# Spreading one row of the first chunk unevenly over the DMA engines, and loading the bias on 16 partitions

## The chip, the cores and the metric

The kernel runs on one core of a Trainium2 chip. The metric is the device time of one execution in microseconds, the median of several runs. A profile is one separate execution, recorded by the hardware; its span runs from the first to the last instruction and is somewhat shorter than the run's time.

## What is computed

A relative position bias is added to attention logits, and a softmax is taken over each row. Everything is float32; there are 2 x 8 matrices of 2112 x 2112.

```python
B, H, S = (2, 8, 2112)
max_rel = 16
rel = pos[:, None] - pos[None, :]
rel_clipped = np.clip(rel, -max_rel, max_rel) + max_rel
bias = rel_bias[:, rel_clipped].copy()          # rel_bias: 8 heads x 33 values
logits = logits + bias[None, :, :, :]
logits = logits - logits.max(axis=-1, keepdims=True)
exp = np.exp(logits)
return (exp / exp.sum(axis=-1, keepdims=True)).astype(np.float32)
```

The bias depends only on the head and on how far a column lies from the row: one of 33 values within 16 columns of the diagonal, and the first or the last of the 33 beyond.

## The kernel before

**Tiling.** All 33792 rows are split over 128 partitions, 264 consecutive rows to each. Eight partitions make one matrix (one batch and head), so partition p belongs to head (p/8) mod 8. A chunk is six rows of every partition (`R = 6`): 128 pieces of 50688 bytes, 6.49 MB. There are 44 chunks and four buffers `X[0]` to `X[3]`, used in turn. A chunk is loaded into a buffer, worked on in place, and stored from it.

**The work of a chunk.** DVE adds the bias and takes the row's maximum in one instruction per row (`add`, L166). ACT takes the exponential with that maximum and sums the row (`exps`, L175). DVE takes the reciprocals of three sums and scales three rows (`scale`, L183 and L187). The bias comes from `F`, a strip of 2135 columns, which DVE copies out of a wider table `M` in PSUM once per four chunks (`strip`, L160); every row reads it at another offset.

**The queues.** SP issues all loads and stores of chunks (`load` L78, `store` L82), in one order written out by hand: first the loads of chunks 0 to 3, then in a loop the store of chunk n+1, a wait until the store of chunk n has landed, and the load of chunk n+4 into the buffer that has become free. The last chunk is stored in two halves. Each transfer raises a semaphore by 16 when all of its parts have landed; `take` waits for a count and subtracts it. A transfer is cut up among 16 DMA engines, which work through their parts in order.

**The start.** The first chunk is not loaded by one transfer but by six, one for each row, over all 128 partitions (L88); the first five raise `pre`, the sixth `ld[0]`. The 8 x 33 bias values are loaded by ACT's queue into the beginning of `F`, the same 264 values on every partition (L97). POOL makes partition and head numbers (L101, L102), DVE makes masks from them (L118 to L128), then waits for the bias (L129), keeps the own head's 33 values with a mask (L131) and adds over the heads (L135), so that `rbS` holds the 33 values of the partition's head; from them it builds the table `M` (L139 to L155). All of these raise one semaphore, `dve`, and `settle` waits until all issued so far are done. Before its loop DVE waits for the five rows (`take(v, pre, ...)`, L190), copies the first strip (L160), waits for the sixth row (L163) and begins to add.

Of the kernel before, what the change touches and what calls it, by code (L numbers as in the profile page):

```python
# [15 lines left out]
def kernel(  # L16
# [6 lines left out]
    nc = tc.nc  # L23
    P = 128
    B, H, S, S2 = logits.shape
    assert S == S2
    MR = 16
    W = 2 * MR + 1
    ROWS = B * H * S // P
    PB = S // ROWS  # L30
    assert ROWS * P == B * H * S and PB * ROWS == S and PB == H == 8
    R = 6
    NBUF = 4
# [4 lines left out]
    MW = S + ROWS - 1  # L38
    FW = S + STEP - 1
    BIG = 3.0e38  # L40

    io = ctx.enter_context(tc.tile_pool(name="io", bufs=1))
    X = [io.tile([P, R * S], FP32, tag=f"X{b}", name=f"X{b}") for b in range(NBUF)]
    F = io.tile([P, FW], FP32, tag="F", name="F")
    rbS = io.tile([P, W], FP32, tag="rbS", name="rbS")
# [3 lines left out]
    ip = io.tile([P, 3, PB], I32, tag="ip", name="ip")  # L49
# [3 lines left out]
    def view(t, offset, dims):  # L53

        return bass.AP(tensor=t.tensor, offset=t.offset + offset, ap=[[list(t.ap[0])[0], P]] + dims)

    def rows(t, j, n):

        return bass.AP(tensor=t.tensor, offset=t.offset + j * S, ap=[[ROWS * S, P], [1, n * S]])

    with tc.tile_critical(no_gpsimd_drain=True):
        ld = [nc.alloc_semaphore(f"ld{b}") for b in range(NBUF)]
# [3 lines left out]
        scaled = nc.alloc_semaphore("scaled")  # L66
        inv = nc.alloc_semaphore("inv")
        rb = nc.alloc_semaphore("rb")
        pre = nc.alloc_semaphore("pre")
        idx = nc.alloc_semaphore("idx")  # L70
        dve = nc.alloc_semaphore("dve")

        def take(eng, sem, n):
            eng.wait_ge(sem, n).then_inc(sem, -n)  # L74


        def load(j, b):
            nc.sync.dma_start(out=X[b][:, :], in_=rows(logits, j, R)).then_inc(ld[b], 16)  # L78
# [5 lines left out]
            ).then_inc(st[b], 16)  # L84


        for r in range(R):
            nc.sync.dma_start(  # L88
                out=X[0][:, r * S : (r + 1) * S], in_=rows(logits, r, 1)
            ).then_inc(ld[0] if r == R - 1 else pre, 16)  # L90
        for n in range(1, NBUF):
            load(n * R, n)

        rbB = view(F, 0, [[1, H * W]])
        nc.scalar.dma_start(  # L97
            out=rbB,
            in_=bass.AP(tensor=rel_bias.tensor, offset=rel_bias.offset, ap=[[0, P], [1, H * W]]),
        ).then_inc(rb, 16)  # L100
        nc.gpsimd.iota(ip[:, 0], pattern=[[0, PB]], base=0, channel_multiplier=1).then_inc(idx, 1)  # L101
        nc.gpsimd.iota(ip[:, 2], pattern=[[1, PB]], base=0, channel_multiplier=0).then_inc(idx, 1)  # L102

        v = nc.vector
        done = [0]

        def then(ins):
            done[0] += 1
            ins.then_inc(dve, 1)

        def settle():
            v.wait_ge(dve, done[0])

        SC = H * W
        mask = [F[:, SC + i * PB : SC + (i + 1) * PB] for i in range(9)]
        dp, dh, eq, hm, gt, le, lt, ra, rz = mask
        v.wait_ge(idx, 2)
        then(v.tensor_scalar(out=ip[:, 1], in0=ip[:, 0], scalar1=3, scalar2=7,  # L118
                             op0=ALU.logical_shift_right, op1=ALU.bitwise_and))
# [7 lines left out]
        for m, op in ((eq, ALU.is_equal), (gt, ALU.is_gt), (le, ALU.is_le), (lt, ALU.is_lt)):  # L127
# [4 lines left out]
            out=view(F, 0, [[W, H], [1, W]]), in0=view(F, 0, [[W, H], [1, W]]),  # L132
            in1=view(F, SC + 3 * PB, [[1, H], [0, W]]), op=ALU.mult))
        settle()
        then(v.tensor_reduce(out=rbS[:, :], in_=view(F, 0, [[1, W], [W, H]]),  # L135
                             axis=mybir.AxisListType.X, op=ALU.add))
        settle()
        low, high = rbS[:, W - 1 : W], rbS[:, 0:1]
        then(v.tensor_scalar(out=ra, in0=gt, scalar1=low, scalar2=None, op0=ALU.mult))  # L139
        then(v.tensor_scalar(out=rz, in0=gt, scalar1=low, scalar2=None, op0=ALU.mult))  # L140
        then(v.tensor_tensor(  # L141
            out=view(F, 0, [[W, PB], [1, W]]), in0=view(F, SC + 2 * PB, [[1, PB], [0, W]]),
            in1=view(rbS, W - 1, [[0, PB], [-1, W]]), op=ALU.mult))
# [6 lines left out]
            out=view(M, U, [[ROWS, PB], [1, W]]), in0=view(F, 0, [[W, PB], [1, W]]),  # L150
            in1=view(F, SC + 8 * PB, [[1, PB], [0, W]]), op=ALU.add))
        then(v.tensor_copy(out=view(M, U + W, [[ROWS, PB], [1, ROWS - W]]),  # L152
                           in_=view(F, SC + 7 * PB, [[1, PB], [0, ROWS - W]])))
        then(v.tensor_copy(out=M[:, 0:U], in_=low.to_broadcast([P, U])))  # L154
# [7 lines left out]
        def add(b):  # L162
            take(v, ld[b], 16)  # L163
            for r in range(b * R, (b + 1) * R):
                x = X[b][:, (r - b * R) * S : (r - b * R + 1) * S]
                v.tensor_tensor_reduce(  # L166
                    out=x, in0=x, in1=F[:, STEP - 1 - r : STEP - 1 - r + S], scale=-1.0, scalar=BIG,
                    op0=ALU.add, op1=ALU.min, accum_out=nmax[:, r : r + 1],
# [18 lines left out]
                    v.tensor_scalar_mul(out=x, in0=x, scalar1=rec[:, r : r + 1]).then_inc(scaled, 1)  # L187

        v.sem_inc(dve, -done[0])
        take(v, pre, 16 * (R - 1))  # L190
        with nc.Fori(0, ROWS - STEP + 1, STEP, engines=[ENG.DVE]) as j:  # L191
            strip(j)
            take(v, dve, 1)
# [51 lines left out]
```

## Time and profile before

| | us |
|---|---|
| Median of 3 runs (1331.09 to 1331.68) | 1331.55 |
| Span of the profiled execution | 1327.7 |
| DVE busy | 976.6 |
| ACT busy | 575.2 |

The profiled execution's own time is not listed beside its span; the runs' median lies 3.85 us above the span. The span is read together with how busy the 16 DMA engines are: the profile gives their mean share and the bytes moved in any window. A packet is what one engine moves in one piece (here one partition's part of a transfer) and is counted in the window in which it starts. In windows of 2 us and less, a long packet at a border shifts the share noticeably. "SPq" and "ACTq" are the instruction queues of SP and ACT, from which transfers are issued.

### The profile page before, as it was taken

The page shows a single profiled execution, that of the slowest core. Times are in us where ns is not written, and L with a number is a line of the kernel's source. Part 1 is how long each engine was busy: PE and PEld are TensorE (multiplying, and loading weights), DVE is VectorE, ACT ScalarE, POOL GpSimd, SP SyncE. Part 2 cuts the span into 40 slices and gives each one's busy share as a digit, 9 for nine tenths or more (in the row PEclk, how much of TensorE's full clock was granted, in tenths as well). Part 3 has the DMA queues.
Part 4 walks back from the last instruction along what each step waited for, and adds up shares of the span by engine and source line. Part 5 has one row for each costly group of instructions (what it writes and reads, how often), then busy time and mean ns, then how long its engine had stood idle before and what let it go on. Part 6 is the DMA issues. An engine that isn't in the chain of part 4 may idle for free. (4 is left out here: it accounts for less than half of the span.)

```text
span 1327.7 us, 2454 instructions
## 1 busy us (share of the span) xinstructions
DVE 976.6 (74%) x911; ACT 575.2 (43%) x539; POOL 0.4 (0%) x6
## 2 busy tenths in 40 slices
DVE  6999667777777776687778777677877776687772
ACT  2564333444444343345444333444444343335440
POOL 0000000000000000000000000000000000000000
DMA  9999999999999999999999999999999999999998
GB/s 392 431 428 437 435 420 437 435 434 425 435 437 434 428 435 434 435 429 429 438 438 432 426 438 437 437 425 437 437 437 425 435 440 437 428 432 438 437 426 359
DMA packets 13683, 571.11 MB, mean 430 GB/s; under 512 B 1521, under 2 KB 1649, under 8 KB 1649
## 3 DMA queue, kind: packets, MB, share of 16 engines
q1 hardware_dynamic: 13536, 570.96, 99.6%
q10 hardware_dynamic: 144, 0.14, 0.1%
q14 instruction: 3, 0.02, 0.0%
HBM read 285.61 MB, written 285.47 MB: 430 GB/s over the span
## 5 line engine op out<-in xcount | busy, mean ns | idle before, releaser
L166 DVE CUSTOM_DVE_ANT_0 X<-X,F 128x2112 f32<-128x2112 f32 x264 | 605.2, 2354 | 301.3 <-DVEq L74 301.3
L175 ACT ACTIVATE X<-X,nmax 128x2112 f32<-128x2112 f32 x264 | 541.7, 2052 | 539.3 <-ACTq L74 517.6
L187 DVE TENSOR_SCALAR X<-X,rec 128x2112 f32<-128x2112 f32 x264 | 332.4, 1315 | 13.2
L175 ACT ACT_TABLE_LOAD x11 | 14.1, 1283 | 183.3 <-ACTq L74 183.3
L175 ACT ACTIVATION_READ_ACCUMULATOR X<-X,nmax 128x1 f32 x264 | 49.2, 186 | 0.0
L160 DVE COPY F<-M 128x2135 f32 x11 | 26.1, 2374 | 6.3 <-DVEq L74 6.3
L166 DVE DVE_READ_ACCUMULATOR2_ANT nmax<- 128x1 f32 x264 | 21.7, 82 | 0.0
L183 DVE RECIPROCAL rec<-tot 128x3 f32<-128x3 f32 x88 | 14.9, 170 | 0.0
L131 DVE TENSOR_TENSOR F<-F 128x264 f32<-128x264 f32 x1 | 0.4, 434 | 4.7 <-DMA F<-in_rel_bias_dram 4.7
L152 DVE COPY M<-F 128x1848 f32<-128x1848 f32 x1 | 2.1, 2077 | 0.0
L118 DVE TENSOR_SCALAR ip<-ip 128x8 int32<-128x8 int32 x1 | 0.2, 173 | 1.3 <-POOL ip L102 1.3
L135 DVE TENSOR_REDUCE rbS<-F 128x33 f32<-128x264 f32 x1 | 0.6, 610 | 0.0
L149 DVE TENSOR_TENSOR M<-F 128x264 f32<-128x264 f32 x1 | 0.4, 441 | 0.0
L141 DVE TENSOR_TENSOR F<-F,rbS 128x264 f32<-128x264 f32 x1 | 0.4, 425 | 0.0
L128 DVE TENSOR_SCALAR F<-F 128x8 f32<-128x8 f32 x4 | 0.4, 166 | 0.0
L154 DVE COPY M<-rbS 128x247 f32<-128x247 f32 x1 | 0.4, 408 | 0.0
L139 DVE TENSOR_SCALAR F<-F,rbS 128x8 f32<-128x8 f32 x1 | 0.2, 231 | 0.0
L145 DVE SCALAR_TENSOR_TENSOR F<-F,rbS 128x8 f32<-128x8 f32 x1 | 0.2, 225 | 0.0
L140 DVE TENSOR_SCALAR F<-F,rbS 128x8 f32<-128x8 f32 x1 | 0.2, 222 | 0.0
L146 DVE SCALAR_TENSOR_TENSOR F<-F,rbS 128x8 f32<-128x8 f32 x1 | 0.2, 219 | 0.0
L124 DVE TENSOR_TENSOR F<-ip 128x8 f32<-128x8 int32 x1 | 0.2, 167 | 0.0
L121 DVE TENSOR_TENSOR F<-ip 128x8 f32<-128x8 int32 x1 | 0.2, 166 | 0.0
(9 smaller groups left out, 1.2 us busy)
## 6 DMA issues: line engine op xcount, KB each, us to landing
X<-in_logits_dram SPq DMA_DIRECT2D x43, 6336.0 KB, 44.6
out_dram<-X SPq DMA_DIRECT2D x43, 6336.0 KB, 52.6
X<-in_logits_dram SPq DMA_DIRECT2D x6, 1056.0 KB, 12.1
out_dram<-X SPq DMA_DIRECT2D x2, 3168.0 KB, 21.1
F<-in_rel_bias_dram ACTq DMA_DIRECT2D x1, 132.0 KB, 6.2
```

The lines of the kernel that those rows point to most:

```text
L128: then(v.tensor_scalar(out=m, in0=dp, scalar1=0.0, scalar2=None, op0=op))
L131: then(v.tensor_tensor(out=view(F, 0, [[W, H], [1, W]]), in0=view(F, 0, [[W, H], [1, W]]), in1=view(F, SC + 3 * PB, [[1, H], [0, W]]), op= ...
L135: then(v.tensor_reduce(out=rbS[:, :], in_=view(F, 0, [[1, W], [W, H]]), axis=mybir.AxisListType.X, op=ALU.add))
L141: then(v.tensor_tensor(out=view(F, 0, [[W, PB], [1, W]]), in0=view(F, SC + 2 * PB, [[1, PB], [0, W]]), in1=view(rbS, W - 1, [[0, PB], [-1, ...
L149: then(v.tensor_tensor(out=view(M, U, [[ROWS, PB], [1, W]]), in0=view(F, 0, [[W, PB], [1, W]]), in1=view(F, SC + 8 * PB, [[1, PB], [0, W]] ...
L152: then(v.tensor_copy(out=view(M, U + W, [[ROWS, PB], [1, ROWS - W]]), in_=view(F, SC + 7 * PB, [[1, PB], [0, ROWS - W]])))
L154: then(v.tensor_copy(out=M[:, 0:U], in_=low.to_broadcast([P, U])))
L160: v.tensor_copy(out=F[:, :], in_=M[:, bass.ds(ROWS - STEP - j, FW)]).then_inc(dve, 1)
L166: v.tensor_tensor_reduce(out=x, in0=x, in1=F[:, STEP - 1 - r : STEP - 1 - r + S], scale=-1.0, scalar=BIG, op0=ALU.add, op1=ALU.min, accum_ ...
L175: nc.scalar.activation(out=x, in_=x, func=EXP, scale=-1.0, bias=nmax[:, r : r + 1], accum_out=tot[:, r : r + 1],).then_inc(expd, 1)
L183: v.reciprocal(out=rec[:, r0 : r0 + HALF], in_=tot[:, r0 : r0 + HALF]).then_inc(inv, 1)
L187: v.tensor_scalar_mul(out=x, in0=x, scalar1=rec[:, r : r + 1]).then_inc(scaled, 1)
```

## The change

The bias is loaded on 16 partitions, one in eight, in place of 128. For that, DVE first clears the 264 columns of `F` on all partitions, and ACT waits for it before it issues the load. The mask and the sum over the heads work as before, and give zeros on partitions without data. Two 32 x 32 block transposes with a copy between them then spread the 33 values of each of the 16 partitions over its group of eight.

The first five rows of the first chunk are one transfer (42240 bytes for each partition), raising `pre`. The sixth row goes in 16 transfers over neighbouring partitions, of 15, 14, and so on down to 8, again 8, and down to 1 partitions. The first eight of them raise `pre`, the next seven `fan`, and the last `ld[0]`. DVE waits for the first two semaphores before its loop, for the last where it waited before. The loads of chunks 1 to 3 follow behind these on SP.

```diff
+    FAN = [15, 14, 13, 12, 11, 10, 9, 8, 8, 7, 6, 5, 4, 3, 2, 1]
...
-        for r in range(R):
-            nc.sync.dma_start(
-                out=X[0][:, r * S : (r + 1) * S], in_=rows(logits, r, 1)
-            ).then_inc(ld[0] if r == R - 1 else pre, 16)
-        for n in range(1, NBUF):
-            load(n * R, n)
-        rbB = view(F, 0, [[1, H * W]])
-        nc.scalar.dma_start(
-            out=rbB,
-            in_=bass.AP(tensor=rel_bias.tensor, offset=rel_bias.offset, ap=[[0, P], [1, H * W]]),
-        ).then_inc(rb, 16)
...
+        then(v.memset(F[:, 0 : H * W], 0.0))
+
+        nc.scalar.wait_ge(dve, 1)
+        nc.scalar.dma_start(
+            out=bass.AP(tensor=F.tensor, offset=F.offset, ap=[[PB * list(F.ap[0])[0], P // PB], [1, H * W]]),
+            in_=bass.AP(
+                tensor=rel_bias.tensor, offset=rel_bias.offset, ap=[[0, P // PB], [1, H * W]]
+            ),
+        ).then_inc(rb, 16)
+        nc.sync.dma_start(
+            out=X[0][:, 0 : (R - 1) * S], in_=rows(logits, 0, R - 1)
+        ).then_inc(pre, 16)
+        p = 0
+        for i, k in enumerate(FAN):
+            nc.sync.dma_start(
+                out=X[0][p : p + k, (R - 1) * S : R * S],
+                in_=bass.AP(
+                    tensor=logits.tensor, offset=logits.offset + (p * ROWS + R - 1) * S,
+                    ap=[[ROWS * S, k], [1, S]],
+                ),
+            ).then_inc(ld[0] if i == len(FAN) - 1 else pre if i < len(FAN) // 2 else fan, 16)
+            p += k
+        for n in range(1, NBUF):
+            load(n * R, n)
...
+        Q = 32
+        RB, RT, RC, RW = [SC + 9 * PB + 2 * Q * i for i in range(4)]
+        then(v.memset(F[:, RB : RB + 2 * Q], 0.0))
...
-        then(v.tensor_reduce(out=rbS[:, :], in_=view(F, 0, [[1, W], [W, H]]),
+        then(v.tensor_reduce(out=F[:, RB : RB + W], in_=view(F, 0, [[1, W], [W, H]]),
                              axis=mybir.AxisListType.X, op=ALU.add))
+        settle()
+        then(v.transpose(out=F[:, RT : RT + 2 * Q], in_=F[:, RB : RB + 2 * Q]))
+        settle()
+        then(v.tensor_copy(out=view(F, RC, [[Q, 2], [PB, Q // PB], [1, PB]]),
+                           in_=view(F, RT, [[Q, 2], [PB, Q // PB], [0, PB]])))
+        settle()
+        then(v.transpose(out=F[:, RW : RW + 2 * Q], in_=F[:, RC : RC + 2 * Q]))
+        settle()
+        then(v.tensor_copy(out=rbS[:, :], in_=F[:, RW : RW + W]))
...
-        take(v, pre, 16 * (R - 1))
+        take(v, pre, 16 * (1 + len(FAN) // 2))
+        take(v, fan, 16 * (len(FAN) - len(FAN) // 2 - 1))
```

More of the change, by code (lines that the diff above doesn't have):

```diff
@@ L40 @@
     BIG = 3.0e38
+    FAN = [15, 14, 13, 12, 11, 10, 9, 8, 8, 7, 6, 5, 4, 3, 2, 1]
+    assert sum(FAN) == P
     io = ctx.enter_context(tc.tile_pool(name="io", bufs=1))
@@ L68 @@
         rb = nc.alloc_semaphore("rb")
-        pre = nc.alloc_semaphore("pre")
         idx = nc.alloc_semaphore("idx")
         dve = nc.alloc_semaphore("dve")
+        pre = nc.alloc_semaphore("pre")
+        fan = nc.alloc_semaphore("fan")
         def take(eng, sem, n):
@@ L84, in store @@
             ).then_inc(st[b], 16)
-        for r in range(R):
-            nc.sync.dma_start(
-                out=X[0][:, r * S : (r + 1) * S], in_=rows(logits, r, 1)
-            ).then_inc(ld[0] if r == R - 1 else pre, 16)
-        for n in range(1, NBUF):
-            load(n * R, n)
-        rbB = view(F, 0, [[1, H * W]])
-        nc.scalar.dma_start(
-            out=rbB,
-            in_=bass.AP(tensor=rel_bias.tensor, offset=rel_bias.offset, ap=[[0, P], [1, H * W]]),
-        ).then_inc(rb, 16)
-        nc.gpsimd.iota(ip[:, 0], pattern=[[0, PB]], base=0, channel_multiplier=1).then_inc(idx, 1)
-        nc.gpsimd.iota(ip[:, 2], pattern=[[1, PB]], base=0, channel_multiplier=0).then_inc(idx, 1)
         v = nc.vector
@@ L112, in settle @@
             v.wait_ge(dve, done[0])
+        then(v.memset(F[:, 0 : H * W], 0.0))
[21 more added lines that the diff above has]
+            load(n * R, n)
+        nc.gpsimd.iota(ip[:, 0], pattern=[[0, PB]], base=0, channel_multiplier=1).then_inc(idx, 1)
+        nc.gpsimd.iota(ip[:, 2], pattern=[[1, PB]], base=0, channel_multiplier=0).then_inc(idx, 1)
         SC = H * W
```

## The prediction, made before the change was run

> **What bounds the kernel now.** I read the page's queue table first, then the waits, then windows of the span, then the start and the end instruction by instruction.
>
> ```profile
> span 1327.7 us, 2454 instructions
> DVE 976.6 (74%) x911; ACT 575.2 (43%) x539; POOL 0.4 (0%) x6
> q1 hardware_dynamic: 13536, 570.96, 99.6%
> q10 hardware_dynamic: 144, 0.14, 0.1%
> ...
> 60.00:1300.00 1240.00, 926.29 (x853) 548.67 (x514) 0.00 (x0) 1.00 1.00 433
> ```
>
> The last row is a window: length, busy time of DVE, ACT and POOL, clock, DMA share, GB/s. SP's queue (q1) keeps the 16 DMA engines busy 99.6% of the span, and from 60 to 1300 us their share is 1.00 at 433 GB/s, which is 27.06 GB/s for one engine. So one row of one partition (8448 bytes) costs an engine 0.312 us, and eight of them, an engine's part of one row of a chunk, 2.50 us. DVE and ACT are never the bound; what they do matters only where it leaves the queue empty. The time is therefore the time of the DMA engine that ends last: start, its bytes, and what it loses on the way. The tail shows how unequal they are:
>
> ```profile
> 1300.00:1320.60 20.60, 3.60 (x3) 0.00 (x0) 0.00 (x0) 1.00 1.00 431
> 1320.60:1321.50 0.90, 0.00 (x0) 0.00 (x0) 0.00 (x0) 1.00 0.40 169
> 1321.50:1324.00 2.50, 0.00 (x0) 0.00 (x0) 0.00 (x0) 1.00 0.45 193
> 1324.00:1325.40 1.40, 0.00 (x0) 0.00 (x0) 0.00 (x0) 1.00 0.21 91
> 1325.40:1326.30 0.90, 0.00 (x0) 0.00 (x0) 0.00 (x0) 1.00 0.00 0
> ```
>
> At 1320.6 us the share falls from 1.00 to 0.40 to 0.45: nine engines have taken their last packet, seven go on, and the last packet is taken before 1325.4. Packets count where they start; those of the last stores (3168 KB over 128 partitions, a row further down) last 25344/27060 = 0.94 us, so the last engine ends near 1326.3, some 5.4 us behind the first. An average engine is 0.40 x 0.9 + 0.45 x 2.5 + 0.21 x 1.4 = 1.8 us behind the first. No view says which of the 16 lag, or when they fell behind. The other loss is at the start:
>
> ```profile
> 0.92 0.41 ACTq L97 DMA_DIRECT2D F<-in_rel_bias_dram  x1
> 0.97 3.34 SPq L88 DMA_DIRECT2D X<-in_logits_dram  x6
> 4.36 1.74 SPq L78 DMA_DIRECT2D X<-in_logits_dram  x3
> ...
> 2.27:4.00 1.73, 0.19 (x3) 0.00 (x0) 0.00 (x0) 1.00 0.99 189
> 4.00:6.00 2.00, 0.00 (x0) 0.00 (x0) 0.00 (x0) 1.00 0.87 280
> 6.00:8.00 2.00, 0.81 (x2) 0.00 (x0) 0.00 (x0) 1.00 0.96 396
> 7.00:19.00 12.00, 5.45 (x12) 0.00 (x0) 0.00 (x0) 1.00 1.01 428
> ```
>
> Against 433 GB/s the first three windows lose 1.73 x (1 - 189/433) + 2 x (1 - 280/433) + 2 x (1 - 396/433) = 0.97 + 0.71 + 0.17 = 1.85 us of every engine. That is when the bias's 128 small packets (q10) run between those of the first row.
>
> **The bias load: 16 packets for 128.** Its 0.14 MB cost 0.14/433 = 0.3 us of all engines; seven eighths go, 0.28 us. If the small packets also caused the 1.85 us beside them, 2.1 us go; if that is only cold starting, none of it. I take 1.2, midway, and keep 0.3 and 2.1. One transfer in place of five saves five rows x 2.50 x (433/428 - 1) = 0.15 us; sixteen transfers end in more semaphore packets and give that back. Sum at the start: -1.2 us for every engine.
>
> **The bias on DVE: nothing.** ACT's issue now waits for a memset of 264 columns. No row shows a memset on DVE; between 0.17 us (8 columns) and 2.08 us (1848) I take the copy of 247 columns, 0.41. A second memset of 64, two transposes of 64 and two copies come on, between 0.17 and 0.43 us each by the narrow rows and L131, so some 1.5 us in all (1.2 to 2.6).
>
> ```profile
> 7.16 0.43 DVE L131 TENSOR_TENSOR F<-F 128x264 f32<-128x264 f32 x1 [4.69 <-DMA F<-in_rel_bias_dram]
> ...
> 9.75 2.08 DVE L152 COPY M<-F 128x1848 f32<-128x1848 f32 x1
> 11.74 0.41 DVE L154 COPY M<-rbS 128x247 f32<-128x247 f32 x1
> 12.06 0.17 DVE L155 COPY M<-rbS 128x16 f32<-128x16 f32 x1
> 18.48 2.38 DVE L160 COPY F<-M 128x2135 f32 x1 [6.26 <-DVEq L74]
> ```
>
> A bias packet may also stand behind two of the first transfer's packets (42240 bytes, 1.56 us each), 3 us more. What hides it all is the 6.26 us that DVE waits before L160 for the first five rows. Those, and the sixth with them now, come no sooner than 15 us, and the setup ends near 12.2 + 0.5 + 1.5, 17 at worst. With the cover gone it costs DVE alone, which has 26% to spare.
>
> **SP's issues: nothing.** Six take 3.34 us, 0.56 each. The loads of chunks 1 to 3 (L78) are moved behind 17 issues: 0.97 + 17 x 0.56 = 10.5 us in place of 4.36. The engines have the five rows until about 2.3 + 12.5 = 14.8 us. An issue would have to cost 0.8 us before an engine ran dry, and those that would run dry first are the ones given fewest packets.
>
> **The sixth row: the term that decides.** Engine 0 is to take 16 packets in place of 8, engine 15 none. At its own pace engine 0 gains 8 x 0.312 = 2.5 us of work, engine 15 loses as much, and the others lie between. That holds if 27.06 GB/s belongs to the engine. Before, every transfer goes over all 128 partitions, so the trace cannot tell the pace of an engine from the pace of the part of SBUF that it writes: 128/16 is eight partitions to a part. If the pace is the part's, fifteen neighbouring partitions written by fifteen engines crowd into few parts, each with one engine's pace to share. How many of a block lie in one part: at least 1, at most 8. I take 4. A packet then costs up to 4 x 0.312 = 1.25 us. Engine 4 is in the twelve transfers of five partitions and more; crowded throughout they cost it 15.0 us, never crowded 3.7. Stepping through all engines' packets in order, with equal shares in a part and the next load's packets taking shares too, I get 12.7 us for engine 4, the worst, against 2.5 before: **+10.2 us**. The same steps give +6.2 with two to a part and +14.9 with eight, and these are my ends. Engine 15 comes out at 0: it runs ahead into chunk 1 and loses that lead to engines which write into its part. [...]
>
> [...]
>
> **What is late next.** The first strip waits for the sixth row now, behind it all of DVE's first chunk, then ACT, then SP's store: at about 14.8 + 12.7 = 27.5 us in place of 18.48, 9 us later.
>
> ```profile
> 43.07 22.23 SPq L82 DMA_DIRECT2D out_dram<-X  x2
> 81.12 0.36 SPq L78 DMA_DIRECT2D X<-in_logits_dram  x1
> ...
> X<-in_logits_dram SPq DMA_DIRECT2D x43, 6336.0 KB, 44.6
> out_dram<-X SPq DMA_DIRECT2D x2, 3168.0 KB, 21.1
> ```
>
> The first store goes from 43.07 to 52 us, while the loads (three of 6336 KB, 6.49 MB, 15.0 us each, behind the first 20 us) keep the engines until 65. The load into the first buffer waits for that store's slowest engine, 81.12 + 9 = 90 us, while the fast engines have the second store until 94. Nothing runs dry, by 4 us; without that cover a late microsecond costs one, of the fast engines, which end early anyway.
>
> **The sum**, for the engine that ends last, from 1326.3 us: back to the first engine's end (-5.4), the start (-1.2), the fan (+10.2), and what the engines then lose on the way, 0 to 5.4, of which I take the average engine's 1.8: +5.4 us. The span would be 1333.1. The profiled execution had 1327.7 in its span, and the runs' median of 1331.55 lies 3.85 above it, which I leave as it is: **1337 us**. With the ends of its terms: 6.2 - 5.4 - 2.1 + 0 = -1.3, and 14.9 - 5.4 - 0.3 + 5.4 = +14.6; all ends seldom fall together, so its own range is 1331 to 1344.
>
> **Rivals.**
>
> *A: the engines keep their own pace, and the laggards are the high numbers.* For it: nine lead and seven lag, as engines 0 to 8 and 9 to 15 would, and a spread of 5.4 us is what sixteen packets make (5.0). Then the last loses about 2.5 and the start 1.2: 1331.55 - 3.7 = 1327.9, faster. It decides if a packet of the fan takes 0.312 us whatever it writes. Against it: nothing shows that the laggards are in the order of their numbers. [...]
>
> *B: own pace, and laggards among the low numbers.* The last engine gets up to 2.5 on top, less 1.2: 1332.9, within the noise.
>
> *C: the change doesn't do what it says.* Either the short transfers are spread over all engines alike, or lags form again from any start. Only the start's gain is left: 1331.55 - 1.2 = 1330.4.
>
> *D: the short transfers go out slowly or through one engine.* At 128 x 0.312 = 40 us in place of 2.5 the last engine would end 37 us later less its spare: 1345 to 1370.
>
> **Chances.** A measurement of this kernel tells 0.2%, 2.7 us, from no change: faster is under 1328.9, slower over 1334.2. Forecast 0.55 (0.49 slower, 0.06 same); A 0.24 (0.20 faster, 0.04 same); B 0.06 (0.04 same, 0.02 slower); C 0.08 (0.06 same, 0.02 faster); D 0.07, slower. Together faster 0.22, same 0.20, slower 0.58. For 8 in 10 I leave out about half of A below, and D with the top of the forecast above: 1327.5 to 1341; the forecast's own range stands beside the sum.
>
> **What would show it.** Windows from 15 to 30 us: under 433 GB/s, losing some 6 us of all engines together, if packets crowd; full if not. The first L160 near 27 us if they crowd, 20 if not. The tail: shares falling in many steps over 10 us if they crowd, under 3 us and a late steep end in A, as before in C. The windows from 2 to 8 us: about 1.2 us less lost, if the bias's packets are to blame. L97's issue later by about 0.5 us, no new wait over 5 us on DVE but the first strip's. The forecast is wrong if the sixth row's windows run full, or if the queue runs dry near 90 us, where the gap would add to the sum.

## The result, and the profile after

The changed kernel takes 1336.93 us (median of 5 runs, 1336.38 to 1337.94) against 1331.3 us before (5 runs, 1329.13 to 1331.68): 5.6 us more. The ratio is 1.0046 with a 95% interval of 1.0034 to 1.0058; it is formed from all the runs and not from the two medians, here and below, and can differ from theirs by up to 0.1%. The profiled execution took 1336.93 us, its span 1335.2.

The page's head and queue table of the changed kernel show the same bound as before, DMA:

```profile
span 1335.2 us, 2472 instructions
...
GB/s 298 435 434 433 434 431 433 434 436 436 433 433 431 434 434 436 434 433 434 431 434 433 436 436 433 434 430 434 434 436 434 436 431 433 434 431 437 434 436 321
...
q1 hardware_dynamic: 13072, 570.96, 99.5%
q10 hardware_dynamic: 32, 0.02, 0.0%
```

The GB/s row has 40 equal slices of the span. All but the first and the last run at full rate; the first, 33 us long, holds the loss (298, against 392 before). In instructions, the start of the changed kernel reads:

```profile
0.97 0.39 SPq L109 DMA_DIRECT2D X<-in_logits_dram  x1
1.40 0.58 ACTq L103 DMA_DIRECT2D F<-in_rel_bias_dram  x1
1.42 5.94 SPq L114 DMA_DIRECT2D X<-in_logits_dram  x16
7.40 1.32 SPq L81 DMA_DIRECT2D X<-in_logits_dram  x3
8.52 0.43 DVE L148 TENSOR_TENSOR F<-F 128x264 f32<-128x264 f32 x1 [6.06 <-DMA F<-in_rel_bias_dram]
14.43 0.17 DVE L181 COPY M<-rbS 128x16 f32<-128x16 f32 x1
29.96 2.38 DVE L186 COPY F<-M 128x2135 f32 x1 [15.37 <-DVEq L77]
...
89.89 0.36 SPq L81 DMA_DIRECT2D X<-in_logits_dram  x1
```

All short transfers are issued by 7.4 us and the table is built by 14.6, yet the first strip waits until 29.96 us for the sixth row. Windows of the changed kernel (length, busy time of DVE, ACT and POOL, clock, DMA share, GB/s) over that time and over the tail:

```profile
16.00:20.00 4.00, 0.00 (x0) 0.00 (x0) 0.00 (x0) 1.00 1.23 194
20.00:24.00 4.00, 0.00 (x0) 0.00 (x0) 0.00 (x0) 1.00 1.20 163
24.00:28.00 4.00, 0.00 (x0) 0.00 (x0) 0.00 (x0) 1.00 0.78 184
...
14.00:30.00 16.00, 0.63 (x4) 0.00 (x0) 0.00 (x0) 1.00 1.00 202
60.00:1300.00 1240.00, 931.10 (x855) 554.10 (x520) 0.00 (x0) 1.00 1.00 434
...
1321.50:1324.00 2.50, 0.00 (x0) 0.00 (x0) 0.00 (x0) 1.00 1.01 436
1324.00:1326.00 2.00, 0.00 (x0) 0.00 (x0) 0.00 (x0) 1.00 0.82 355
1326.00:1328.00 2.00, 0.00 (x0) 0.00 (x0) 0.00 (x0) 1.00 0.47 203
1328.00:1330.00 2.00, 0.00 (x0) 0.00 (x0) 0.00 (x0) 1.00 0.18 76
1330.00:1332.00 2.00, 0.00 (x0) 0.00 (x0) 0.00 (x0) 1.00 0.06 25
1332.00:1334.00 2.00, 0.00 (x0) 0.00 (x0) 0.00 (x0) 1.00 0.03 13
```

From 14 to 30 us the engines are busy (share 1.00) and move 202 GB/s: their packets are slow, they are not idle (the sixth row's 128 have a median of 0.83 us in the trace, in place of 0.32 before). Against 433 GB/s that loses 16 x (1 - 202/433) = 8.5 us of an average engine. The tail has another shape than before: there is no cliff with seven laggards behind it. The engines end one by one over 5 us, and a single one (0.06 is one engine of 16) goes on for 3 us more.

### The profile page after: what moved, and what is told of

Read it like the earlier page. It is cut to its first block, busy times and chain, and to the rows that moved or that the text cites. A ratio compares the mean times of both kernels' runs of the same rounds, so it can differ in the third digit from the quotient of the medians.

```text
span 1335.2 us, 2472 instructions
## 1 busy us (share of the span) xinstructions
DVE 977.8 (73%) x917; ACT 575.2 (43%) x539; POOL 0.4 (0%) x6
```

## The experiments

Four things were to be told apart: whether the bias or the fan (the sixteen short transfers of the sixth row) costs the time; whether the fan costs by its uneven shares, by the number of its short transfers, or by the neighbouring partitions; if the neighbours, on which side; and which engines lag. Each run's medians go with those of the kernel before on the same chip in the same session.

**The parts alone.** First the bias on 16 partitions, with the six one-row transfers of before; then all of the change but the fan.

```diff
-        nc.sync.dma_start(
-            out=X[0][:, 0 : (R - 1) * S], in_=rows(logits, 0, R - 1)
-        ).then_inc(pre, 16)
-        for i, k in enumerate(FAN):
...
+        for r in range(R):
+            nc.sync.dma_start(
+                out=X[0][:, r * S : (r + 1) * S], in_=rows(logits, r, 1)
+            ).then_inc(ld[0] if r == R - 1 else pre, 16)
```

> The bias on 16 partitions with its transposes, and the first chunk in six one-row transfers as before: the sixth row is not fanned out. Crowding theory (the fan alone costs time, the bias load gains at the start): the start's gain is left, 1 to 1.7 us less than before, 1329.6 to 1330.3 us. Rival (the bias's waits and transposes cost time, or its 112 packets fewer gain nothing): 1331.3 us or more, and the first landings of the first row no earlier than before.

```diff
-        for i, k in enumerate(FAN):
...
+        nc.sync.dma_start(
+            out=X[0][:, (R - 1) * S : R * S], in_=rows(logits, R - 1, 1)
+        ).then_inc(ld[0], 16)
```

> The changed kernel with the sixth row in one transfer over all 128 partitions in place of sixteen short ones; all else as changed. Crowding theory: the whole loss goes, 1329 to 1330.5 us, and no window between 14 and 30 us falls under 420 GB/s. Rival (the other parts, the later first strip or the bias, make the loss): still 1334 us or more.

The bias alone took 1332.95 us against 1331.16 (1.0013, 1.0004 to 1.0022); without the fan it was 1332.08 against 1331.16 (1.0005, 0.9996 to 1.0014). So the fan is what costs: 5.6 us over before with it, 0.9 without, 4.7 between. But the gain forecast from the bias never reached the end. It is there at the start. Here are the same windows as before, and the first strip, in the run with the bias alone:

```profile
2.27:4.00 1.73, 0.19 (x3) 0.00 (x0) 0.00 (x0) 1.00 0.77 293
4.00:6.00 2.00, 0.00 (x0) 0.00 (x0) 0.00 (x0) 1.00 1.03 418
6.00:8.00 2.00, 1.09 (x3) 0.00 (x0) 0.00 (x0) 1.00 1.02 423
```

```profile
16.84 2.38 DVE L176 COPY F<-M 128x2135 f32 x1 [3.93 <-DVEq L76]
```

The first strip starts at 16.84 us in place of 18.48, and the three windows lose 0.56 + 0.07 + 0.05 = 0.7 us where they lost 1.85. The bias's packets are fewer, and they also start later (at 5.3 us in the trace in place of 2.0); which of the two helps was not separated. The tail of the run without the fan tells where it went:

```profile
1320.00:1321.50 1.50, 0.00 (x0) 0.00 (x0) 0.00 (x0) 1.00 0.43 186
1321.50:1324.00 2.50, 0.00 (x0) 0.00 (x0) 0.00 (x0) 1.00 0.35 152
1324.00:1326.00 2.00, 0.00 (x0) 0.00 (x0) 0.00 (x0) 1.00 0.35 152
1326.00:1328.00 2.00, 0.00 (x0) 0.00 (x0) 0.00 (x0) 1.00 0.15 63
1328.00:1330.00 2.00, 0.00 (x0) 0.00 (x0) 0.00 (x0) 1.00 0.00 0
```

The leading engines are done before 1320.5 us, sooner than before; the last by some 1329, later than before's 1326.3. By the landing records in the trace (the moment at which each engine's part of a transfer raises the semaphore) the sixteen parts of the last store land between 1319.9 and 1329.0 us, against 1320.9 and 1326.6 before. The laggards fell further behind.

**Neighbours, with even shares.** The sixth row in eight transfers of 16 partitions, side by side or eight apart: every engine has its eight packets, as in one transfer (in the change's trace the short transfers of 15 to 1 partitions leave one landing for each partition, beside one early landing each, so a packet goes to each of as many engines). The diff is the one side by side; eight apart it has `p0 = i`, and 8 in place of the 1 in both patterns.

```diff
-        for i, k in enumerate(FAN):
...
+        for i in range(8):
+            p0 = 16 * i
+            xa = X[0]
             nc.sync.dma_start(
...
+                out=bass.AP(
+                    tensor=xa.tensor, offset=xa.offset + p0 * list(xa.ap[0])[0] + (R - 1) * S,
+                    ap=[[1 * list(xa.ap[0])[0], 16], [1, S]],
+                ),
                 in_=bass.AP(
...
+                    tensor=logits.tensor, offset=logits.offset + (p0 * ROWS + R - 1) * S,
+                    ap=[[1 * ROWS * S, 16], [1, S]],
                 ),
...
```

> The changed kernel with the sixth row in eight transfers of 16 neighbouring partitions each, so every engine takes eight packets of it, as in one whole transfer. Crowding theory, four to a part of SBUF: a packet takes 4 x 0.312 us, the row 10 us in place of 2.5, all engines late by 7.5 alike, against the start's gain 1331.3 - 1.5 + 7.5 = 1337 us. Rival one (engines at their own pace, only unevenness costs): 1329.8 us. Rival two (each short transfer costs an engine a fixed 0.85 us, the mean length of the fan's packets, wherever it writes): 8 x 0.85 = 6.8 us in place of 2.5, 1334 us.

> As the run with 16 neighbours, but the 16 partitions of a transfer lie eight apart, from one end of SBUF to the other. Crowding theory: one or two to a part in place of four, so 0 to 2.5 us late, 1329.8 to 1332.3 us, some 5 to 7 us under the run with neighbours, though the transfers are as many and as large. Rival one (own pace): 1329.8 us, like the neighbours. Rival two (a fixed cost for each short transfer): 1334 us, like the neighbours.

Measured: 1333.91 us (1.0021, 1.0011 to 1.0030) side by side, 1332.35 (0.9999, 0.9990 to 1.0008) eight apart, 1331.16 before. Windows of the one, then of the other:

```profile
14.00:30.00 16.00, 7.37 (x9) 2.09 (x2) 0.00 (x0) 1.00 1.02 329
```

```profile
14.00:30.00 16.00, 8.91 (x8) 3.74 (x4) 0.00 (x0) 1.00 1.04 380
```

They lose 16 x (1 - 329/433) = 3.8 and 2.0 us, where the whole transfer of the run without the fan loses 0.2 (428 GB/s). So neighbours cost with even shares too, and the engine's own pace (no loss in either) falls. The size was missed: 7.5 us was expected of the neighbours, and 1337 us in all. The packets eight apart last 0.64 us at most in the trace (median 0.61), twice the 0.312 us of an engine at its pace; those side by side have a median of 0.79 us, not 1.25. The medians are only 1.6 us apart, so the windows and the packets carry the reading.

**Neighbours, with uneven shares.** Sixteen transfers of eight partitions, so that eight engines, called 0 to 7, take all 128 packets, side by side or four apart: the same loop, with 8 partitions for 16 in the patterns. Against the run with 16 neighbours, side by side; four apart it has `p0 = 32 * (i // 4) + i % 4`, and 4 in place of the 1 in both patterns.

```diff
-        for i in range(8):
-            p0 = 16 * i
+        for i in range(16):
+            p0 = 8 * i
...
```

> The changed kernel with the sixth row in sixteen transfers of eight neighbouring partitions, so engines 0 to 7 take 16 packets of it and engines 8 to 15 none. Crowding theory: a transfer goes to two parts, four packets to each, 16 x 4 x 0.312 = 20 us and more where the next load's packets share a part, some 20 us late for the lower eight: 1331.3 - 1.5 + 20 = 1350 us. Rival one (own pace): 16 x 0.312 = 5.0 us, 2.5 late, 1332.3 us at most. Rival two (0.85 us for each short transfer): 13.6 us, 11 late, 1341 us.

> As the run with eight neighbours, but the eight partitions of a transfer lie four apart. The same packets on the same engines. Crowding theory: each packet of a transfer in a part of its own, sharing only with the next load's packets of the upper eight engines: 7.5 us in place of 2.5, 5 late, 1335 us. Rival one (own pace): 1332.3 us, like the neighbours. Rival two (a fixed cost for each short transfer): 1341 us, like the neighbours.

Measured: 1340.18 us (1.0064, 1.0045 to 1.0082) and 1332.70 (1.0011, 1.0002 to 1.0021), 1331.08 before. These are sixteen transfers of one size, with the same number of packets on the same engines, and the times are 7.5 us apart. Windows, side by side and then four apart, and the first strip of the latter:

```profile
14.00:30.00 16.00, 0.70 (x3) 0.00 (x0) 0.00 (x0) 1.00 1.03 174
```

```profile
14.00:30.00 16.00, 6.32 (x7) 1.02 (x1) 0.00 (x0) 1.00 1.00 360
```

```profile
23.81 2.38 DVE L189 COPY F<-M 128x2135 f32 x1 [9.37 <-DVEq L77]
```

A fixed price for each short transfer (1341 us for both) falls. Four apart, the sixth row's last packet ends at 23.0 us in the trace, 7.2 after the last of the five rows, where 7.5 was expected. Its packets last 0.32 us in the first half of that time, when partitions 0 to 63 are written, and 0.63 in the second, for 64 to 127: one and two times 0.312 us. The expectation had the next load's packets of the other eight engines take a share too; that they are what doubles the second half was not shown. Side by side 20 us (1350 in all) were expected and some 14 came: again the loss is milder than four equal shares would make it. It also reaches the eight engines that have no share of the row: their first packets of the next load, begun near 15.5 us, last 3.9 to 4.4 us side by side and 1.9 to 2.1 four apart.

**Which side.** These are the same two runs with one side exchanged: written side by side but read from the rows of partitions four apart, and the reverse. The sixth row of the first chunk then holds other rows' data. The diff is the first of them, against the run with eight neighbours.

```diff
-            p0 = 8 * i
+            p0, q0 = 8 * i, 32 * (i // 4) + i % 4
...
-                    tensor=logits.tensor, offset=logits.offset + (p0 * ROWS + R - 1) * S,
-                    ap=[[1 * ROWS * S, 8], [1, S]],
+                    tensor=logits.tensor, offset=logits.offset + (q0 * ROWS + R - 1) * S,
+                    ap=[[4 * ROWS * S, 8], [1, S]],
```

> The sixth row in sixteen transfers of eight, written to eight neighbouring partitions, but read from the rows that belong to partitions four apart, so that row of the first chunk holds other rows' data. With neighbours on both sides it was 1340 us, with four apart on both 1333. If the crowding is where the engines write (SBUF): 1340 us, the load of chunk 1 landing near 46 us. If it is where they read (neighbouring partitions' rows in HBM): 1333 us, landing near 39 us. If each side makes a part: between.

> The reverse: written four apart, read from the rows that belong to eight neighbours; that row of the first chunk holds other rows' data. Crowding where the engines write: 1333 us, the load of chunk 1 landing near 39 us. Crowding where they read: 1340 us, landing near 46 us.

Measured: 1338.83 us written side by side (1.0065, 1.0049 to 1.0080), 1332.75 written four apart (1.0019, 1.0010 to 1.0029), 1330.23 before. Their windows in that order:

```profile
14.00:30.00 16.00, 0.72 (x3) 0.00 (x0) 0.00 (x0) 1.00 1.02 199
```

```profile
14.00:30.00 16.00, 6.18 (x6) 1.15 (x1) 0.00 (x0) 1.00 0.97 346
```

The times follow the side that is written, and so do the landings of chunk 1 in the landing records: 44.8 us written side by side and 38.6 written four apart. So the crowding is on the side that is written, SBUF; the rows' places in HBM account for about a microsecond (199 against 174 GB/s).

**The change, spread out.** The same sixteen transfers of 15 to 1 and 8 partitions, in the same order, each over partitions eight apart.

```diff
         for i, k in enumerate(FAN):
+            o = i if i < 8 else 15 - i
+            p0 = o if i < 8 else o + 8 * (16 - k)
+            xa = X[0]
             nc.sync.dma_start(
-                out=X[0][p : p + k, (R - 1) * S : R * S],
+                out=bass.AP(
+                    tensor=xa.tensor, offset=xa.offset + p0 * list(xa.ap[0])[0] + (R - 1) * S,
+                    ap=[[8 * list(xa.ap[0])[0], k], [1, S]],
+                ),
...
```

> The change itself with the same sixteen transfers of 15 to 1 and 8 partitions in the same order, but the partitions of each lie eight apart, not side by side. The engines' numbers of packets are the same. If neighbours are what costs: the load of chunk 1 lands some 3 to 5 us sooner than in the change (44.75 us there) and the time falls to 1332 to 1334 us. If the short transfers or the uneven shares cost whatever they touch: 1336 to 1338 us, as the change.

It took 1333.94 us (1.0029, 1.0018 to 1.0040; 1330.23 before), 3.0 us less than the change, or 1.9 less with each held against before in its own session, and its window and first strip:

```profile
14.00:30.00 16.00, 3.66 (x4) 0.00 (x0) 0.00 (x0) 1.00 1.00 288
```

```profile
26.29 2.38 DVE L190 COPY F<-M 128x2135 f32 x1 [12.03 <-DVEq L77]
```

5.4 us lost in place of 8.5, and by the landing records chunk 1 landed 3.6 us sooner (41.1 against 44.75 us). Both are within what was expected of the neighbours; taken against before in its own session, though, the gain of 1.9 us puts the time at 1335, between the two forecasts. The rest of the fan's cost stays when it is spread out: its packets have a median of 0.62 us, twice 0.312.

**Which engines end last.** Fifteen tiny loads of 1 to 15 partitions behind the last store, each followed by a small copy on ACT that waits for it.

```diff
+        for k in range(1, 16):
+            nc.sync.dma_start(
+                out=PR[0:k, k : k + 1],
+                in_=bass.AP(tensor=logits.tensor, offset=logits.offset, ap=[[ROWS * S, k], [1, 1]]),
+            ).then_inc(pb[k], 16)
+        for k in range(1, 16):
+            nc.scalar.wait_ge(pb[k], 16)
+            nc.scalar.copy(out=PQ[0:1, k : k + 1], in_=PR[0:1, k : k + 1])
```

> The kernel before with fifteen tiny loads issued behind the last store, of 1 to 15 partitions (four bytes each), and an instruction of ACT behind each, which starts when the engines that this load uses have done all before it. If a load of k partitions runs on the lowest k engines, the starts climb with k and each step up shows an engine that ends later than all below it. Theory of the change's numbers (laggards are high): flat near 1321 us up to k = 9, then up to 1326. Rival (laggards among the low numbers): near 1324 to 1326 from a small k on. The time itself is to stay within 2 us of before.

> The changed kernel with the same fifteen tiny loads at its end. Crowding theory: the engines with many packets of the fan end last, so the start behind the first load is already late, within 3 us of the last. Own pace with engine 0 last: the first start is the last. If the lags form again from any start: the same steps at the same k as in the kernel before.

One run each was made, at 1330.71 and 1338.42 us. A load of k partitions leaves k landings in the trace, and each longer load adds one to those of the shorter; engine k here is the one that the load of k + 1 partitions adds. These are ACT's copies in the timeline (start, duration, idle time before and what ended it), in the kernel before and then in the changed one:

```profile
1320.84 0.19 ACT L223 COPY PQ<-PR 1x1 f32<-1x1 f32 x1 [22.24 <-DMA PR<-in_logits_dram]
1321.91 0.36 ACT L223 COPY PQ<-PR 1x1 f32<-1x1 f32 x2 [0.88 <-DMA PR<-in_logits_dram]
1325.01 0.19 ACT L223 COPY PQ<-PR 1x1 f32<-1x1 f32 x1 [2.73 <-DMA PR<-in_logits_dram]
1325.96 2.10 ACT L223 COPY PQ<-PR 1x1 f32<-1x1 f32 x11 [0.76 <-DMA PR<-in_logits_dram]
```

```profile
1330.01 0.72 ACT L250 COPY PQ<-PR 1x1 f32<-1x1 f32 x4 [26.20 <-DMA PR<-in_logits_dram]
1333.68 2.08 ACT L250 COPY PQ<-PR 1x1 f32<-1x1 f32 x11 [2.96 <-DMA PR<-in_logits_dram]
```

Before, engines 0 to 2 are done by 1321.9 us; the load of four partitions steps up to 1325.0 and that of five to 1326.0, so engines 3 and 4 lag. The other eleven copies run back to back, and ACT can't separate them; the trace's landing records of the loads, taken one by one, add engines 10 to 14, and engine 15 by elimination. So in this execution the laggards were mostly, not only, high numbers. After, engine 0 is late at 1330.0, and engine 4 alone is last at 1333.7; the landing records of the others fall, with one exception, from engine 0 to engine 14, from 1330 to 1325. Engine 4 is the one that the prediction's steps made the worst. But it was among the laggards of the kernel before too, and the last landing is 1.0 us behind the next at chunk 1 and 3.6 at the end, so this does not show that the fan alone made it last.

**A milder spread.** Partitions 0 to 63 of the sixth row in eight transfers four apart on engines 0 to 7, the rest in one over all 16: 12 packets against 4. The loop is as above, with n partitions from p0, st_ apart.

```diff
+        for i in range(9):
+            p0, st_, n = (32 * (i // 4) + i % 4, 4, 8) if i < 8 else (64, 1, 64)
...
```

> A milder unevenness: of the sixth row, partitions 0 to 63 go in eight transfers of eight four apart (engines 0 to 7), partitions 64 to 127 in one transfer over all 16 engines, so that engines 0 to 7 take 12 packets of it and 8 to 15 take 4: 2.5 us between them in place of 5. If a spread of 5 us at the start is what kept the engines from falling behind later, and half does too: little loss on the way, 1329 to 1330.5 us, under both kernels. If half is not enough: engines fall behind as with no spread, 1331.5 to 1333 us.

It took 1332.20 us against 1330.23 (1.0017, 1.0008 to 1.0026), the second of the two forecasts: not under the kernel before. No version tried beats it.

## Why the prediction came out

The time was forecast at 1337 and is 1336.93. The likeliest case, crowding, is the one that happened, but the closeness is partly luck. The sum was made against the profiled execution and 3.85 us were added for what lies around the span. In every later run that has both numbers, 1.7 to 2.1 us lie around it; the execution profiled before, at 1327.7, was one of the quick ones. So the sum's +5.4 should have been held against 1335.2 - 1327.7 = +7.5, and two errors of 2 us cancelled. The landing records give the sum's own steps: back to the first engine's end, -5.6 us (forecast -5.4); the start and the fan together, from the first landing of chunk 1 before, 34.75, to the last one after, 44.75, +10.0 (forecast -1.2 + 10.2 = +9.0); on the way +2.6 (forecast +1.8). Together that is +7.0. Term by term:

- **The bound.** Right: DMA before and after, 433 and 434 GB/s between 60 and 1300 us.
- **The start, -1.2.** Right at the start, where the bias alone gives 1.2 us in the windows and 1.6 at the first strip. Without the fan it did not reach the end: the leaders end sooner and the last engine later, and the time is no shorter. Here an early start of all engines was not yet an early end of the last one.
- **DVE's and SP's part, nothing.** Right. The bias's issue is 0.48 us later, the table is done at 14.6 us (14.2 forecast), and the four added steps are hidden behind the wait for the sixth row. SP's issues were cheaper than taken, 0.37 us each.
- **The fan, +10.2 for the last engine.** The cause is right (1340.18 us side by side, 1332.70 four apart), and the size nearly. That four of a block share a part was the author's estimate, and no run shows it: written side by side, the packets have a median of 0.79 us with 16 partitions to a transfer and 0.83 in the change, where four equal shares make 1.25. For the last engine, chunk 1 lands at 44.75 us in the changed kernel (7.40 + 37.4 from issue to landing) against 33.8 without the fan (1.88 + 32.0), 10.9 later. The changed kernel's issue at 7.40 stands above; here are the landings of its loads of chunks 1 to 3, then, without the fan, their issue and landings (chunk 1 is the minimum):

```profile
DMA to landing us min/median/max: 37.4/51.9/66.4
```

```profile
1.88 1.73 SPq L80 DMA_DIRECT2D X<-in_logits_dram  x3
```

```profile
DMA to landing us min/median/max: 32.0/46.7/62.2
```

- **Its spread.** Wrong: engine 15 was to come out at 0. By the landing records the first engine is 6.9 us late (39.9 against 33.0), and the average lost 8.5 where the steps gave some 6. In the trace the next load's first packets, on engines that were done with the fan or had none of it, last some 5 us in place of 1.87 from 16 to 24 us (14 packets, 4.7 to 6.1). Equal shares fit the packets written apart, which last one and two times 0.312 us (0.32 and 0.63 four apart, 0.61 eight apart), and not those written side by side: there the packets themselves do better (0.79 in place of 1.25 us), and the engines that are already in the next load do worse than the steps have it. How neighbours slow them wasn't settled.
- **On the way, +1.8.** The last engine lost 2.6 us more than the first of before did from chunk 1 on; the range of 0 to 5.4 held it. The reason given, an average engine's lag, was not the reason: taken in their order of landing, eleven engines of the changed kernel need 1285.7 to 1285.9 us from chunk 1 to the end, four lose up to 1.1 us on that and one loses 3.
- **What is late next.** Right: first strip at 29.96 (27.5 forecast), the load into the first buffer at 89.89 (90), no dry queue there (share 1.00 from 60 to 1300 us).
- **Rivals.** A and B fell with the own pace, though A's laggards were mostly real. C falls, since the sixteen transfers do go unevenly over the engines (the landings of chunk 1 lie 4.9 us apart, 0.8 before); its second half, lags that form again from any start, falls too: only one engine lags in the changed kernel. D falls: the last engine ended 7 us later, not 37.

## What to carry to other kernels

Here a transfer's cost depended on which partitions it wrote at once, not only on how many packets each engine got (1340.18 us side by side against 1332.70 four apart, with the same packets): with the change's row cut into blocks of neighbours, the engines moved less than half the rate (202 of 433 GB/s). If work has to be moved between engines, try each short transfer's partitions spread out, and compare at the last engine's end: the gain of 1.2 us for all engines at the start was gone by then. Take the offset between span and time from runs that have both.

## What had not been expected

In these traces several engines that start together fall behind later; of engines that start 5 us apart, hardly more than one does. From the landing of chunk 1 to that of the last store (landing records in the trace), the average engine needs 1287.9 us in the kernel before, 1289.3 with the bias alone, 1289.6 without the fan and 1288.2 to 1288.4 in the two runs with 16 partitions to a transfer; in all of these chunk 1 lands within 0.9 us on the sixteen, and five to seven engines end 3 to 9.5 us behind the first. It needs 1286.2 us in the change and 1286.2 to 1286.3 in the others with a spread of 4.6 to 5.5 us, and 1287.6 with 2.8. So of the 8.5 us that the fan lost, the average engine got 1289.6 - 1286.2 = 3.4 back, while the time rose by 4.7 us over the kernel without it. But the average does not set the time: in every run with such a spread the last engine still loses 3 to 5 us on the way, and none of these runs came under the kernel before. Why engines in step fall behind was not tried.

Transfers with a step between their partitions cost SP more to issue in these runs. These rows are of the runs with the fan eight apart and with eight partitions four apart; the change's sixteen take 5.94 us:

```profile
1.42 11.79 SPq L116 DMA_DIRECT2D X<-in_logits_dram  x16
```

```profile
1.43 10.82 SPq L115 DMA_DIRECT2D X<-in_logits_dram  x16
```

That is 0.7 us each in place of 0.37. It was still early enough here: the load of chunk 1 was issued at 13.3 us at the latest, before the five rows had landed.
